# A two-block model on one core: norm gains by a product, early vectors, a split gate block, and ordered modulation additions

## The chip, the cores and the metric

The kernel runs on one core of a Trainium2 chip. The core has a matrix engine (TensorE, PE in the rows; its weight loads are PEld), VectorE (DVE), ScalarE (ACT), GpSimd (POOL) and SyncE (SP), which here issues almost all DMAs, in order. The metric is the device time of one execution in microseconds. The kernel before took 2379.94 us (median of three runs, 2379.12 to 2382.21). Where a clock is given, it is the share of TensorE's full speed that was granted in a stretch: 1.00 is 2.4 GHz, 0.50 is 1.2 GHz, and a value between them is a mixture of the two.

## What is computed

A first block with two layers (an even and an odd one) over 256 latent and 256 context tokens of width 1024 is followed by a second block. The change lies in the even layer and in helpers that all layers use. The even layer modulates a normed input, multiplies it with one wide matrix, and runs window attention and a gated linear recurrence (HGRN) on the parts:

```python
def even_mixer(h_ctx, h_lat, w_in, w_out, qk_g, sink, out_g, lb, cos, sin, need_ctx):
    p = split_parts(h_lat @ w_in, EVEN_PARTS)     # a_q a_k a_v b_q b_ff b_fb b_i b_g
    pc = project_parts(h_ctx, w_in, EVEN_PARTS, names)
...
    k_ctx = kv_heads(pc['a_k'], qk_g[1])          # rms_norm of each 64-wide head, times qk_g
    q_lat = apply_rope(attn_q_heads(p['a_q'], qk_g[0]), cos, sin)
    k_lat = apply_rope(kv_heads(p['a_k'], qk_g[1]), cos, sin)
    a_lat = window_attention(q_lat, k_lat, kv_heads(p['a_v']), k_ctx, v_ctx, sink)
...
    o_fw, _ = gla_chunked(q_l, k_fw, i_l, lf_fw, s_fw)          # 4 heads of 128
    o_bw, _ = gla_chunked(flip(q_l), flip(k_bw), flip(i_l), flip(lf_bw), s_bw)
    b_lat = gated_head_norm(o_fw + flip(o_bw), p['b_g'], out_g)  # rms_norm * out_g * silu(b_g)
    y_lat = jnp.concatenate([a_lat.astype(dt), b_lat.astype(dt)], axis=-1) @ w_out

def modulate(h, shift, scale):                    # shift, scale: chunks of silu(c) @ mod_w + mod_b
    return h * (1.0 + scale) + shift
```

Each layer ends with a gated FFN (`swiglu`) behind a second modulated norm. The modulation vectors are the products of two condition vectors with a 1024x6144 matrix for each layer (`mod_w`, and `w_ada` in the second block).

## The kernel before, in words

All products run as three matmuls of high and low parts (`mm3`, L188 to L190). A weight tile comes by `wload` (L176 ff.): SP loads `raw`, ScalarE casts it to `whi`, VectorE or (every fourth) GpSimd subtracts to `wlo`; four buffers of each. A tile scheduler orders each engine's instructions by priority, and the five engines meet by semaphores.

The even layer begins in `layer_even` (L1066). Rows of x and ctx are loaded, normed and transposed to `xT`. `modulate_first` (L1086) goes over the model width in four parts q, here called pairs, since each covers two chunks of 128: eight loads of mod_w (`mbig`, L1107, a buffer pool that holds two pairs), PE products of them with the conditions (L1112), the bias added on VectorE (`mrow`, L1118), a transposition (L1120), the modulation coefficients `firsta` and `firstb`, and the modulated operand chunks hi and lo. After each pair `first_products` (L1136) multiplies the two chunks with their rows of the weights. At q equal to 2 two DMAs spread the head-norm gains over all partitions (`qkg`, L1116). Ahead of pair 0 stand the loads of the norm vectors (L318) and of the modulation bias (`mbias`, L1097).

`even` (L706) then prepares q and k (`even_prep`, L945), makes gates for head pair 0 (`gates_in`), the values (`proj_narrow` with BI), and interleaves the four HGRN heads (`hgrn_head`, L823) with attention (`even_attention`, L989) by a string of steps; at the step g it makes the gates of pair 1. At the end the gates b_g are made (`ev_g`), multiplied with the gain `ogain` on GpSimd (L792), and with the heads' outputs on VectorE and GpSimd (L800), and PE transposes the products (L801). Then come the residual rows' transpositions (L1062) and the out projection.

The modulation vectors of later norms are summed in small pieces between other work: `mod_sums` (L364) loads a piece of 128x512 (`mraw`, four buffers), and VectorE adds it, scaled by a condition, to `macc` (L382). `fill` (L394), called by every `mm3`, advances it at a set rate. At a norm, `norm_sums` and `norm_spread` (L548 ff.) make the row norms and spread them over `nrs`; the first weight blocks of the FFN or of the next layer run on unnormed operands, and VectorE applies nrs to their results (`scaled`, L600, tile `nu`), while `normed` (L608) makes the normed operands: `nt` (L618), its high part on ScalarE, its low part `hTl` (L620).

Of the kernel before, what the change touches and what calls it, by code (L numbers as in the profile page):

```python
# [11 lines left out]
F32 = mybir.dt.float32  # L12
# [3 lines left out]
ALU = mybir.AluOpType  # L16
# [3 lines left out]
P = 128  # L20
D = 1024
# [74 lines left out]
class Net:  # L96
    def __init__(self, ctx, tc, I, out):
        self.ctx, self.tc, self.nc, self.I, self.out = ctx, tc, tc.nc, I, out
        self.n = 0
        e = ctx.enter_context  # L100
        self.cp = e(tc.tile_pool(name="cp", bufs=1, reuse_waits="tile"))
        self.wp = e(tc.tile_pool(name="wp", bufs=2))
        self.st = e(tc.tile_pool(name="st", bufs=4))
        self.mpool = e(tc.tile_pool(name="mp", bufs=1, reuse_waits="tile"))
        self.gran, self.pool_every = 0, 4
        self.credit, self.rate, self.todo = 0, 0, iter(())

# [173 lines left out]
    def setup(self):  # L281
        nc, I = self.nc, self.I
        self.vidx, self.vc = {}, self.t(self.cp, [P, 96], tag="vcols")
        flat = lambda a: a.rearrange("l (k p) -> (l k) p", p=P)
        self.vectors({"c": flat(I["c"]), "cc": I["c_ctx"].rearrange("(k p) -> k p", p=P), "c2": flat(I["c_2"])}, first=True)
        self.neghalf = self.t(self.cp, [P, 40], tag="neghalf")
        nc.gpsimd.memset(self.neghalf, -0.5)
        self.half = self.t(self.cp, [P, 4], tag="half")
        nc.gpsimd.memset(self.half, 0.5)
        self.ones2 = self.t(self.cp, [P, 2], tag="ones2")  # L290
        nc.gpsimd.memset(self.ones2, 1.0)
        self.onesq = self.t(self.cp, [P, P], tag="onesq")
        nc.gpsimd.memset(self.onesq, 1.0)

        sil = self.t(self.cp, [P, 24], tag="sil")
        nc.scalar.activation(sil, self.vc[:, 0:24], AF.Silu)
        self.cond = self.t(self.cp, [P, 8, 32], tag="cond")
        nc.gpsimd.memset(self.cond, 0.0)
        for m in range(2):
            nc.vector.tensor_copy(self.cond[:, :, m], sil[:, m * 8:m * 8 + 8])  # L300
        self.vs = [sil[:, o:o + 8] for o in (0, 8, 16)]
# [62 lines left out]
    def mod_sums(self, M, r):  # L364
# [6 lines left out]
        for g0 in range(0, 4, step):  # L371
            gs, accs = range(g0, g0 + step), {}
            for g in gs:
                for m in range(len(vs)):
                    accs[g, m] = self.t(self.mod_pool, [P, 512], tag="macc", bufs=4)
                for k in range(8):
# [3 lines left out]
                    for m, v in enumerate(vs):  # L380
                        if k:
                            nc.vector.scalar_tensor_tensor(accs[g, m], raw, v[:, k:k + 1], accs[g, m], ALU.mult, ALU.add)  # L382
                        else:
                            nc.scalar.activation(accs[g, m], raw, AF.Copy, scale=v[:, 0:1])
# [223 lines left out]
    def normed(self):  # L608
# [3 lines left out]
        with self.urgent():  # L612
            for k in range(8):
                for m, x in enumerate(self.nx):
# [4 lines left out]
                    nc.scalar.activation(hi[:, k, c], t, AF.Identity, bias=b)  # L619
                    nc.vector.scalar_tensor_tensor(lo[:, k, c], t, b, hi[:, k, c].bitcast(F32), ALU.add, ALU.subtract)  # L620
        self.ns.close()
# [84 lines left out]
    def even(self, products, ps, M, load, follow):  # L706
# [6 lines left out]
        with pool("ev") as op, ExitStack() as es:  # L713
# [7 lines left out]
            def gates_in(pair):  # L721
# [4 lines left out]
                for i, c0 in enumerate((BFF, BFB, BQ)):  # L726
                    wt = self.wfm(w, c0 + pair * 256)
                    for fb in range(2):
                        pa = self.acc()
                        self.fm_block(h, 0, 512, wt, fb, pa)  # L730
                        nc.scalar.activation(sg[fb][:, i] if i < 2 else q[fb], pa, AF.Copy, scale=1.0 if i < 2 else 0.5)
            hs = ExitStack()
            with pool("at") as ap:
                kT = self.t(ap, [P, 2, 2, 512], F32R, tag="kT")
                av = self.t(ap, [P, 4, P], tag="av")
                with pool("pp2") as pp, ps:
                    raw = products.send(av)
                    ke = self.const(op, "even")
                    imask = self.const(op, "imask")
                    self.setup_rest()  # L740
                    self.even_prep(pp, ke, raw, qT, kT)
# [12 lines left out]
                nc.vector.tensor_scalar(hi2, lb, 0.5, 0.5, ALU.mult, ALU.add)  # L754
                gates_in(0)
                with tc.high_priority(-1200):
                    for r in (1, 2):
                        self.mod_round(M, r, op)
                self.proj_narrow(h, TBS, w, BI, 512, lambda tb, c, pa: nc.scalar.copy(v[:, tb, c], pa))
                hp = hs.enter_context(pool("hg", side="right"))  # L760

                for nm, n in (("St", 896), ("A1", 1024), ("Bp1", 1024)):
                    self.t(hp, [P, n], tag=nm)
                with pool("sa") as sp:
                    head = lambda hd: self.hgrn_head(hp, ke, imask, hd, *src[hd], lo2, hi2, v)
                    heads = {0: head(0), 1: head(1)}
                    at = self.even_attention(sp, qT, kT, av, [2, 3, 0, 1])
                    for st in "000aa0aaag01111aa022aa12aaaa1aa33aa2aaaa2aa233a33":
                        if st == "a":
                            next(at, None)  # L770
                        elif st == "g":
                            with tc.high_priority(-800):
                                gates_in(1)
                            heads.update({2: head(2), 3: head(3)})
# [7 lines left out]
            with hs:  # L782
                gain = self.bcast_rows(yp, I["hgrn_out_norm_g"][0], P, "ogain")
                nc.vector.tensor_scalar(gain, gain, 0.5, None, ALU.mult)
# [203 lines left out]

    def even_attention(self, ap, qT, kT, av, tbs):  # L989

        nc, tc, I = self.nc, self.tc, self.I
        sink = self.bcast_rows(ap, I["attn_sink"][0], 8, "sink")
        nsink = self.t(ap, [P, 8], tag="nsink")
# [72 lines left out]
    def layer_even(self, M, load):  # L1066
# [7 lines left out]
        self.scratch([], None)  # L1074
        self.qkg = self.t(pp, [P, 10, 64], tag="qkg")
        xT = self.t(self.npool, [P, 8, 512], tag="xT")
        for tb in TBS:
            for i, pt in enumerate(self.norm_rows(src[tb], self.npool)):
                (self.nc.vector.tensor_copy if i else self.nc.scalar.copy)(xT[:, i * 4:i * 4 + 4, tb * P:tb * P + P], pt.rearrange("p (k t) -> p k t", t=P))
        first = self.modulate_first(M, xT)  # L1080
        products = self.first_products(first, I["even_w_in"][0], pp)
# [4 lines left out]
    def modulate_first(self, M, xT):  # L1086

        nc, I, cond = self.nc, self.I, self.cond
        flat = lambda a: a.rearrange("l (k p) -> (l k) p", p=P)
        self.vectors({"ng": I["norm_g"].rearrange("l s (k p) -> (l s k) p", p=P), "nm": flat(I["norm_mix_2"]),  # L1090
                      "nf": flat(I["norm_ffn_2"]), "lb": flat(I["hgrn_lb"])})
        gain = self.vcol("ng", 0)
        bias = self.t(self.npool, [P, 4, P], tag="mbias")
        nc.gpsimd.memset(bias, 0.0)
        for s in range(2):
            for m in range(2):
                nc.sync.dma_start(bias[s * 64:s * 64 + 64].rearrange("(j c) q n -> j c q n", c=32)[:, m],  # L1097
                                  M["bias"][s * D:s * D + D].rearrange("(q j n) -> j q n", j=2, n=P))
        A, B = (self.t(self.npool, [P, 8, 2], tag=nm) for nm in ("firsta", "firstb"))
        (hi, lo), h = self.fm_tiles()  # L1100
        for q in range(4):
            pa = self.bank("mod")
            for k0 in range(0, 8, 2):
# [4 lines left out]
                for i in range(2):  # L1108
                    for s in range(2):
                        for j in range(2):  # L1110
                            g = 64 * s + 32 * j
                            nc.tensor.matmul(pa[g:g + 32, :P], lhsT=cond[:, k0 + i], rhs=raw[:, i, s, j * P:j * P + P],  # L1112
                                             start=k0 + i == 0, stop=k0 + i == 7)
            if q == 2:
                for i, n0, n1 in ((0, 0, 8), (1, 8, 10)):
                    nc.sync.dma_start(self.qkg[:, n0:n1], I["attn_qk_norm_g"][0, i].unsqueeze(0).unsqueeze(0).to_broadcast([P, n1 - n0, 64]))  # L1116
            row = self.t(self.npool, [P, P], tag="mrow", bufs=2)
# [875 lines left out]
```

## Time and profile before

| | |
|---|---|
| median of three runs | 2379.94 us (2379.12 to 2382.21) |
| the profiled execution | 2377.75 us, its span 2375.9 us |
| busy: PE, DVE, ACT, POOL | 2258.2 (95%), 1612.3 (68%), 1064.4 (45%), 761.3 us (32%) |
| bytes moved | 396.70 MB, mean 167 GB/s |
| granted clock over the span | 0.978 |

The profile is of one execution. The first 400 of the 2376 us hold the first block's even layer up to its FFN. A busy share is an average over stretches with different limits, so the table of stretches below is the place to begin: a stretch in which PE is busy throughout has PE as its limit, one with holes has the work that the holes wait for. In a row of waits or of the timeline, the part in square brackets is the time for which the engine stood idle before that instruction, and what ended it.

### The profile page before, as it was taken

To read this page: it belongs to the slowest core of one execution; us is meant where nothing else is said; L and a number is where in the kernel's file an instruction comes from. 1 tells how busy PE (TensorE), PEld (TensorE's weight loads), DVE (VectorE), ACT (ScalarE), POOL (GpSimd) and SP (SyncE) were. 2 spreads that over 40 slices of the span, in tenths; PEclk is the share of its full clock that TensorE was granted. 3 is DMA by queue.
4 is the path that set the end of the run, shared out by engine and by line. 5 is a ranking of instruction groups with operands and counts; after the bars stand their busy time and mean duration, and the time that the engine had idled before them with its cause. 6 is when DMAs were issued, how large, how long until landed. Compare 5 with 4: busy or idle time off the path is not lost. (4 is left out here: it accounts for less than half of the span.)

```text
span 2375.9 us, 41450 instructions
## 1 busy us (share of the span) xinstructions
PE 2258.2 (95%) x16308; PEld 2018.6 (85%) x16308; DVE 1612.3 (68%) x2583; ACT 1064.4 (45%) x1754; POOL 761.3 (32%) x565
## 2 busy tenths in 40 slices
PE   6989989999999899988999899999999889999999
PEld 5767668777778788878999788999999788999999
DVE  2677858775557856568845978548765887548773
ACT  3555524332224433335445654445444655445443
POOL 1454432111012122213444663223223555224221
PEclk9989999999999999999999989999999999999999
DMA  7433335576666557575855634345666544355554
GB/s 247 147 102 113 125 114 161 157 225 209 192 196 210 182 175 238 153 232 171 281 184 167 177 89 121 115 151 162 187 182 185 160 130 114 107 148 172 178 182 138
DMA packets 352423, 396.70 MB, mean 167 GB/s; under 512 B 33916, under 2 KB 297004, under 8 KB 350180
## 3 DMA queue, kind: packets, MB, share of 16 engines
q1 hardware_dynamic: 350052, 393.92, 53.7%
q8 instruction: 128, 2.10, 0.4%
q14 instruction: 67, 0.55, 0.1%
q10 hardware_dynamic: 2176, 0.13, 0.1%
HBM read 390.28 MB, written 3.70 MB: 166 GB/s over the span
## 5 line engine op out<-in xcount | busy, mean ns | idle before, releaser
L180 ACT CAST whi<-raw 128x1024 fp32r<-128x1024 f32 (+2 forms) x536 | 551.5, 1034 | 598.3 <-PE acc L189 387.0
L182 POOL TENSOR_TENSOR wlo<-raw,whi 128x1024 fp32r<-128x1024 f32 (+1 forms) x168 | 411.0, 2446 | 1082.3 <-ACT whi L180 991.7
L188 PE MATMUL acc<-hTh,whi 128*128 128x256 f32 (+2 forms) x2256 | 693.0, 309 | 13.4 <-DVE nu L600 8.0
L182 DVE TENSOR_TENSOR wlo<-raw,whi 128x1024 fp32r<-128x1024 f32 (+1 forms) x368 | 482.0, 1310 | 329.1 <-ACT whi L180 328.1
L189 PE MATMUL acc<-hTl,whi 128*128 128x256 f32 (+2 forms) x2256 | 695.1, 309 | 7.7 <-DVE hTl L620 7.7
L190 PE MATMUL acc<-hTh,wlo 128*128 128x256 f32 (+2 forms) x2256 | 695.1, 309 | 4.3 <-DVE wlo L182 4.3
L188 PEld LDWEIGHTS acc<-hTh,whi 128*128 128x128 f32 x2256 | 430.5, 191 | 43.0 <-issue 9.8
L189 PEld LDWEIGHTS acc<-hTl,whi 128*128 128x128 f32 x2256 | 430.8, 191 | 31.0 <-DVE hTl L620 10.0
L190 PEld LDWEIGHTS acc<-hTh,wlo 128*128 128x128 f32 x2256 | 431.7, 191 | 28.7 <-DVE wlo L182 5.1
L382 DVE SCALAR_TENSOR_TENSOR macc<-mraw,sil,macc 128x512 f32<-128x512 f32 x280 | 249.2, 899 | 72.4 <-DMA mraw<-in_w_ada_dram 35.4
L189 PE MATMUL acc<-hidl,whi 128*128 128x256 f32 (+1 forms) x704 | 218.1, 310 | 0.0
L190 PE MATMUL acc<-hidh,wlo 128*128 128x256 f32 (+1 forms) x704 | 217.7, 310 | 0.0
L188 PE MATMUL acc<-hidh,whi 128*128 128x256 f32 (+1 forms) x704 | 217.6, 310 | 0.0
L188 PE MATMUL acc<-whi,hTh 128*128 128x512 f32 (+2 forms) x560 | 193.6, 347 | 6.8 <-DVE nu L600 2.2
L189 PE MATMUL acc<-wlo,hTh 128*128 128x512 f32 (+2 forms) x560 | 190.3, 341 | 2.7 <-POOL wlo L182 2.6
L190 PE MATMUL acc<-whi,hTl 128*128 128x512 f32 (+2 forms) x560 | 186.8, 343 | 2.8 <-DVE hTl L620 2.2
L188 PEld LDWEIGHTS acc<-hidh,whi 128*128 128x128 f32 x704 | 132.2, 188 | 9.7 <-issue 1.7
L190 PEld LDWEIGHTS acc<-hidh,wlo 128*128 128x128 f32 x704 | 132.6, 188 | 7.9
L189 PEld LDWEIGHTS acc<-hidl,whi 128*128 128x128 f32 x704 | 132.6, 188 | 7.9
L188 PEld LDWEIGHTS acc<-whi,hTh 128*128 128x128 f32 x560 | 107.2, 192 | 28.2 <-issue 8.1
L190 PEld LDWEIGHTS acc<-whi,hTl 128*128 128x128 f32 x560 | 105.8, 191 | 18.7 <-DVE hTl L620 4.4
L189 PEld LDWEIGHTS acc<-wlo,hTh 128*128 128x128 f32 x560 | 107.0, 191 | 15.6 <-POOL wlo L182 3.1
(559 smaller groups left out, 3787.0 us busy)
## 6 DMA issues: line engine op xcount, KB each, us to landing
raw<-in_w_in_dram SPq DMA_DIRECT2D x112, 512.0 KB
mraw<-in_w_ada_dram SPq DMA_DIRECT2D x192, 256.0 KB
raw<-in_ffn_w_in_dram SPq DMA_DIRECT2D x88, 512.0 KB
raw<-in_w_up_dram SPq DMA_DIRECT2D x88, 512.0 KB
mraw<-in_mod_w_dram SPq DMA_DIRECT2D x96, 256.0 KB
raw<-in_odd_w_in_dram SPq DMA_DIRECT2D x48, 512.0 KB
raw<-in_ffn_w_out_dram SPq DMA_DIRECT2D x40, 512.0 KB
raw<-in_w_down_dram SPq DMA_DIRECT2D x40, 512.0 KB
```

Source lines behind the costliest of these rows:

```text
L180: nc.scalar.copy(hi, raw)
L182: eng.tensor_tensor(lo, raw, hi.bitcast(F32), ALU.subtract)
L188: mm(out, lhsT=ah, rhs=bh, start=start, stop=False)
L189: mm(out, lhsT=ah, rhs=bl, start=False, stop=False)
L190: last = mm(out, lhsT=al, rhs=bh, start=False, stop=stop)
L382: nc.vector.scalar_tensor_tensor(accs[g, m], raw, v[:, k:k + 1], accs[g, m], ALU.mult, ALU.add)
```

## The change

The head-norm gains come as one row of 128 numbers into a zeroed 128x128 tile (`qkrow`); a product with a matrix of ones spreads it over the partitions, and two copies on ScalarE write `qkg`. The norm vectors and the modulation bias are issued behind the eight `mbig` loads of pair 0 instead of ahead of them. The broadcasts of `ogain` and `sink` move from where they are used to the constants ahead of `even_prep`. `gates_in` becomes a generator; its first third for pair 1 (BFF, two weight tiles, 48 products) is made right behind the values, the rest at the step g as before. `normed` records its last low-part instruction as `fence`, and each VectorE addition of `mod_sums` that is issued later is ordered behind it. A column tile (`neghalf`) shrinks from 40 to 16 columns.

```diff
@@ mod_sums
                         if k:
-                            nc.vector.scalar_tensor_tensor(accs[g, m], raw, v[:, k:k + 1], accs[g, m], ALU.mult, ALU.add)
+                            add = nc.vector.scalar_tensor_tensor(accs[g, m], raw, v[:, k:k + 1], accs[g, m], ALU.mult, ALU.add)
+                            if self.fence is not None:
+                                self.after(add, self.fence)
@@ normed
-                    nc.vector.scalar_tensor_tensor(lo[:, k, c], t, b, hi[:, k, c].bitcast(F32), ALU.add, ALU.subtract)
+                    self.fence = nc.vector.scalar_tensor_tensor(lo[:, k, c], t, b, hi[:, k, c].bitcast(F32), ALU.add, ALU.subtract)
@@ even: gates_in, constants, values, heads
+                    yield
...
                     imask = self.const(op, "imask")
+                    gain = self.bcast_rows(op, I["hgrn_out_norm_g"][0], P, "ogain")
+                    sink = self.bcast_rows(op, I["attn_sink"][0], 8, "sink")
...
-                gates_in(0)
+                for _ in gates_in(0):
+                    pass
...
                 self.proj_narrow(h, TBS, w, BI, 512, lambda tb, c, pa: nc.scalar.copy(v[:, tb, c], pa))
+                gates = gates_in(1)
+                next(gates)
...
                             with tc.high_priority(-800):
-                                gates_in(1)
+                                for _ in gates:
+                                    pass
...
             with hs:
-                gain = self.bcast_rows(yp, I["hgrn_out_norm_g"][0], P, "ogain")
@@ even_attention
-        sink = self.bcast_rows(ap, I["attn_sink"][0], 8, "sink")
@@ layer_even
+        qk = self.t(pp, [P, 2, 64], tag="qkrow")
+        self.nc.gpsimd.memset(qk, 0.0)
+        self.nc.sync.dma_start(qk[0:1], I["attn_qk_norm_g"])
...
+        pq = self.sm()[:, :P]
+        self.nc.tensor.matmul(pq, lhsT=self.onesq, rhs=qk.rearrange("p a d -> p (a d)"), start=True, stop=True)
+        for i, n0, n1 in ((0, 0, 8), (1, 8, 10)):
+            self.nc.scalar.copy(self.qkg[:, n0:n1], pq[:, i * 64:i * 64 + 64].unsqueeze(1).to_broadcast([P, n1 - n0, 64]))
@@ modulate_first
-            if q == 2:
-                for i, n0, n1 in ((0, 0, 8), (1, 8, 10)):
-                    nc.sync.dma_start(self.qkg[:, n0:n1], I["attn_qk_norm_g"][0, i].unsqueeze(0).unsqueeze(0).to_broadcast([P, n1 - n0, 64]))
+            if q == 0:
+                self.vectors({"ng": I["norm_g"].rearrange("l s (k p) -> (l s k) p", p=P), "nm": flat(I["norm_mix_2"]),
+                              "nf": flat(I["norm_ffn_2"]), "lb": flat(I["hgrn_lb"])})
+                gain = self.vcol("ng", 0)
...
```

How this moves instructions is seen at three places. On SP, in the even layer's prologue; mbig is mod_w, raw from L176 a weight tile. Before:

```order
L1107 DMA mbig_498<-in_mod_w_dram 128x2x256 x2
L1107 DMA mbig_509<-in_mod_w_dram 128x2x256 x2
L1116 DMA qkg_113<-in_attn_qk_norm_g_dram 128x8x64
L1116 DMA qkg_113<-in_attn_qk_norm_g_dram 128x2x64
L176 DMA raw_540<-in_even_w_in_dram 128x2x512
L1107 DMA mbig_571<-in_mod_w_dram 128x2x256 x2
```

And now, where the same two mbig loads are followed by the weight tile at once:

```order
L1114 DMA mbig_505<-in_mod_w_dram 128x2x256 x2
L1114 DMA mbig_516<-in_mod_w_dram 128x2x256 x2
L176 DMA raw_545<-in_even_w_in_dram 128x2x512
L1114 DMA mbig_576<-in_mod_w_dram 128x2x256 x2
L1114 DMA mbig_587<-in_mod_w_dram 128x2x256 x2
```

The two qkg loads are gone from between them. On VectorE at the even FFN's norm (macc is a modulation addition, nt a normed operand, nu the first results scaled). Before:

```order
L563 TENSOR_SCALAR nsum_3746<-k_ident_79,rr_628_3743 128x128 x4
L382 SCALAR_TENSOR_TENSOR macc_4087<-mraw_4182,sil_92,macc_4087 128x512
L382 SCALAR_TENSOR_TENSOR macc_4086<-mraw_4199,sil_92,macc_4086 128x512
L182 TENSOR_TENSOR wlo_4063<-raw_4060,whi_4062 128x1024
L382 SCALAR_TENSOR_TENSOR macc_4212<-mraw_4227,sil_92,macc_4212 128x512
L382 SCALAR_TENSOR_TENSOR macc_4087<-mraw_4199,sil_92,macc_4087 128x512
L382 SCALAR_TENSOR_TENSOR macc_4213<-mraw_4227,sil_92,macc_4213 128x512
L618 SCALAR_TENSOR_TENSOR nt_3992<-x_3228,moda_3438,nrs_3780 128x256
```

And now:

```order
L565 TENSOR_SCALAR nsum_3751<-k_ident_79,rr_630_3748 128x128 x4
L620 SCALAR_TENSOR_TENSOR nt_3997<-x_3233,moda_3443,nrs_3785 128x256
L620 SCALAR_TENSOR_TENSOR nt_4001<-c_3261,moda_3445,nrs_3785 128x256
L620 SCALAR_TENSOR_TENSOR nt_4005<-x_3233,moda_3443,nrs_3785 128x256
L620 SCALAR_TENSOR_TENSOR nt_4009<-c_3261,moda_3445,nrs_3785 128x256
L602 TENSOR_TENSOR nu_3787<-acc_3712,nrs_3785 128x256
```

No addition stands between nsum and nt any more; the same additions follow behind the norm's operands, in runs of 9 to 12 with single weight tiles between them. On GpSimd at the end of the even stage (sg is a gate block, sq a head's output, rv and rr the last head's row norms). Before, all multiplications with ogain stand together, ahead of the first gated output and of the last head's norm:

```order
L792 TENSOR_TENSOR sg_519_2924<-sg_519_2924,ogain_2921 128x256 x2
L792 TENSOR_TENSOR sg_520_2925<-sg_520_2925,ogain_2921 128x256 x2
L792 TENSOR_TENSOR sg_519_2924<-sg_519_2924,ogain_2921 128x256 x2
L792 TENSOR_TENSOR sg_520_2925<-sg_520_2925,ogain_2921 128x256 x2
L800 TENSOR_TENSOR sq_177_921<-sq_177_921,sg_519_2924 128x128
L800 TENSOR_TENSOR sq_178_922<-sq_178_922,sg_519_2924 128x128
L159 TENSOR_SCALAR rv_514_2907<-ss_513_2905 128x4
```

And now only the last head's norm and its gated outputs are left there, behind the last of the attention's softmax rows (P):

```order
L800 TENSOR_TENSOR sg_522_2930<-sg_522_2930,ogain_756 128x256
L1023 TENSOR_SCALAR P_2606<-P_2606,es_478_2609 128x512
L407 MEMSET mraw_1236 128x512
L159 TENSOR_SCALAR rv_517_2914<-ss_516_2912 128x4
L533 MEMSET bz_585_3447 128x16
L533 MEMSET bz_586_3452 128x16
L161 TENSOR_TENSOR rr_518_2916<-rv_517_2914,neghalf_84 128x4
L808 TENSOR_TENSOR sq_252_1481<-sq_252_1481,sg_521_2929 128x128
L808 TENSOR_TENSOR sq_252_1481<-sq_252_1481,sg_522_2930 128x128
```

On PE the transpositions of the first two heads' gated outputs accordingly stand ahead of the last head's products, and the early third of pair 1's gates stands right behind the values, but behind the product that waits for `A` (L882 before, L890 now), which has kept its place.

## Rows read from the trace of the kernel before

**Rows 1.** The page: the span of the profiled execution.
```profile
span 2375.9 us, 41450 instructions
```
**Rows 2.** Stretches: length, busy PE PEld DVE ACT POOL, granted clock, DMA share, GB/s.
```profile
59.40:137.50 78.10, 66.44 (x411) 53.51 (x412) 57.44 (x80) 43.70 (x73) 42.70 (x25) 0.92 0.41 133
137.50:310.60 173.10, 172.04 (x1360) 127.93 (x1358) 126.72 (x305) 83.10 (x184) 77.53 (x62) 0.99 0.37 119
310.60:334.70 24.10, 14.63 (x97) 10.68 (x97) 14.71 (x33) 5.08 (x11) 11.02 (x21) 0.79 0.28 95
...
399.35:440.00 40.65, 39.81 (x207) 33.21 (x208) 40.50 (x75) 21.27 (x41) 3.23 (x3) 0.95 0.50 154
440.00:800.00 360.00, 356.98 (x1639) 287.79 (x1637) 233.79 (x318) 116.42 (x176) 54.96 (x34) 1.00 0.63 198
```
**Rows 3.** Timeline of SP's queue, 31 to 45 us: start, duration of the issue, what.
```profile
31.30 2.11 SPq L1116 DMA_DIRECT2D qkg<-in_attn_qk_norm_g_dram  x2
33.45 1.14 SPq L176 DMA_DIRECT2D raw<-in_even_w_in_dram  x1
34.69 9.77 SPq L1107 DMA_DIRECT2D mbig<-in_mod_w_dram  x1
```
**Rows 4.** Busy time by stretch, prologue, columns as in the second group.
```profile
30.00:36.00 6.00, 6.00 (x43) 4.52 (x43) 2.74 (x3) 1.14 (x2) 0.00 (x0) 1.00 0.98 305
36.00:46.00 10.00, 9.63 (x96) 7.85 (x95) 2.90 (x8) 2.08 (x4) 0.00 (x0) 1.00 0.14 34
...
52.40:59.40 7.00, 3.15 (x13) 2.79 (x14) 1.42 (x4) 2.03 (x5) 2.17 (x1) 0.74 1.06 360
```
**Rows 5.** Timeline of VectorE, 44 to 64 us.
```profile
48.12 0.29 DVE L1118 TENSOR_TENSOR mrow<-mod,mbias 128x128 f32<-128x128 f32 x1 [7.81 <-PE mod L1112]
```
**Rows 6.** Timeline of PE, 30 to 64 us.
```profile
36.94 0.27 PE L1120 MATMUL mod<-k_ident,mrow 128*128 128x128 f32 x1
...
39.02 0.50 PE L188 MATMUL acc<-whi,hTh 128*128 128x512 f32 x1
...
62.13 0.61 PE L188 MATMUL acc<-whi,hTh 128*128 128x512 f32 x1
62.58 0.39 PE L189 MATMUL acc<-wlo,hTh 128*128 128x512 f32 x1
62.80 0.40 PE L188 MATMUL acc<-whi,hTh 128*128 128x512 f32 x1
```
**Rows 7.** Waits of PE, 100 to 140 us: total, times, longest (us).
```profile
PE rc L882 <- DVE A L864: 8.5, 1, 8.5
```
**Rows 8.** Timeline of POOL, 316 to 328 us.
```profile
317.33 5.70 POOL L792 TENSOR_TENSOR sg<-sg,ogain 128x256 f32<-128x256 f32 x8 [3.66 <-DVE ogain L784]
```
**Rows 9.** Waits of PE, 310 to 336 us.
```profile
PE sm L801 <- POOL sq L800: 6.9, 3, 4.9
```
**Rows 10.** Timeline of PE, 328 to 335 us.
```profile
328.74 0.47 PE L801 MATMUL sm<-k_ident,sq 128*128 128x128 f32 x1 [1.85 <-POOL sq L800]
...
334.71 0.48 PE L188 MATMUL acc<-qT,whi 128*128 128x512 f32 x1
```
**Rows 11.** Timeline of ACT, 393 to 395 us.
```profile
394.04 0.59 ACT L575 COPY nrs<-sm 128x512 f32<-128x512 f32 x1
```
**Rows 12.** Groups of VectorE's instructions, 378 to 412 us: count, busy us, mean ns.
```profile
L382 DVE SCALAR_TENSOR_TENSOR macc<-mraw,sil,macc 128x512 f32<-128x512 f32 x28 | 21.5, 815 | 0.4 <-DMA mraw<-in_mod_w_dram 0.3
```
**Rows 13.** Timeline of VectorE, 392 to 400 us.
```profile
393.13 4.16 DVE L382 SCALAR_TENSOR_TENSOR macc<-mraw,sil,macc 128x512 f32<-128x512 f32 x3 [0.27 <-DMA mraw<-in_mod_w_dram]
397.21 0.47 DVE L618 SCALAR_TENSOR_TENSOR nt<-x,moda,nrs 128x256 f32<-128x256 f32 x1
...
398.79 1.07 DVE L600 TENSOR_TENSOR nu<-acc,nrs 128x256 f32<-128x256 f32 x3
```
**Rows 14.** Timeline of PE, 392 to 402 us.
```profile
399.35 0.55 PE L188 MATMUL acc<-hTh,whi 128*128 128x258 f32 x1 [5.35 <-DVE nu L600]
```
**Rows 15.** Waits of PE, 440 to 830 us.
```profile
PE acc L188 <- DVE nu L600: 3.2, 3, 1.3
```

More of the change, by code (lines that the diff above doesn't have):

```diff
@@ L105, in __init__ @@
         self.gran, self.pool_every = 0, 4
-        self.credit, self.rate, self.todo = 0, 0, iter(())
+        self.credit, self.rate, self.todo, self.fence = 0, 0, iter(()), None
     def t(self, pool, shape, dtype=F32, tag=None, bufs=None):
@@ L285, in setup @@
         self.vectors({"c": flat(I["c"]), "cc": I["c_ctx"].rearrange("(k p) -> k p", p=P), "c2": flat(I["c_2"])}, first=True)
-        self.neghalf = self.t(self.cp, [P, 40], tag="neghalf")
+        self.neghalf = self.t(self.cp, [P, 16], tag="neghalf")
         nc.gpsimd.memset(self.neghalf, -0.5)
@@ L766, in even @@
                     heads = {0: head(0), 1: head(1)}
-                    at = self.even_attention(sp, qT, kT, av, [2, 3, 0, 1])
+                    at = self.even_attention(sp, sink, qT, kT, av, [2, 3, 0, 1])
                     for st in "000aa0aaag01111aa022aa12aaaa1aa33aa2aaaa2aa233a33":
@@ L987, in even_prep, with even_attention @@
                 nc.vector.tensor_copy(qT[:, half * 4:half * 4 + 4, tb * P:tb * P + P], pq.rearrange("p (h t) -> p h t", t=P))
-    def even_attention(self, ap, qT, kT, av, tbs):
+    def even_attention(self, ap, sink, qT, kT, av, tbs):
         nc, tc, I = self.nc, self.tc, self.I
-        sink = self.bcast_rows(ap, I["attn_sink"][0], 8, "sink")
         nsink = self.t(ap, [P, 8], tag="nsink")
@@ L1089, in modulate_first @@
         flat = lambda a: a.rearrange("l (k p) -> (l k) p", p=P)
-        self.vectors({"ng": I["norm_g"].rearrange("l s (k p) -> (l s k) p", p=P), "nm": flat(I["norm_mix_2"]),
-                      "nf": flat(I["norm_ffn_2"]), "lb": flat(I["hgrn_lb"])})
-        gain = self.vcol("ng", 0)
         bias = self.t(self.npool, [P, 4, P], tag="mbias")
         nc.gpsimd.memset(bias, 0.0)
[L1095 to L1098, printed above, removed]
         A, B = (self.t(self.npool, [P, 8, 2], tag=nm) for nm in ("firsta", "firstb"))
@@ L1113, in modulate_first @@
                                              start=k0 + i == 0, stop=k0 + i == 7)
-            if q == 2:
-                for i, n0, n1 in ((0, 0, 8), (1, 8, 10)):
-                    nc.sync.dma_start(self.qkg[:, n0:n1], I["attn_qk_norm_g"][0, i].unsqueeze(0).unsqueeze(0).to_broadcast([P, n1 - n0, 64]))
+            if q == 0:
+                self.vectors({"ng": I["norm_g"].rearrange("l s (k p) -> (l s k) p", p=P), "nm": flat(I["norm_mix_2"]),
+                              "nf": flat(I["norm_ffn_2"]), "lb": flat(I["hgrn_lb"])})
+                gain = self.vcol("ng", 0)
+                for s in range(2):
+                    for m in range(2):
+                        nc.sync.dma_start(bias[s * 64:s * 64 + 64].rearrange("(j c) q n -> j c q n", c=32)[:, m],
+                                          M["bias"][s * D:s * D + D].rearrange("(q j n) -> j q n", j=2, n=P))
             row = self.t(self.npool, [P, P], tag="mrow", bufs=2)
```

## The prediction

> **What bounds the kernel now.** I read the span first [rows 1], then a table of busy time by stretch, then the waits of each stretch in which TensorE (PE) has a hole, and last what the queues do in it. The table [rows 2] shows where the even layer's holes are: between 59.4 and 137.5 us PE is busy 66.44 of 78.1 us, between 310.6 and 334.7 only 14.63 of 24.1 us at a granted clock of 0.79, while 137.5 to 310.6 (172.04 of 173.1) and 440 to 800 (356.98 of 360) are full. A step that ends earlier in a full stretch carries its gain to the end, and an instruction that a full stretch gets in addition costs its duration.
>
> The prologue before 59.4 has a hole of its own. SP issues the two qkg loads at 31.30 and then needs 9.77 us for the issue of one mbig load [rows 3]. What the core moves falls from 305 GB/s (30 to 36) to 34 GB/s (36 to 46), while PE still lives on what landed before (9.63 of 10 us busy); later, from 52.4 to 59.4, PE is busy 3.15 of 7 us, at a clock of 0.74 [rows 4]. The weights that lie behind the two loads on SP, the casts that wait for them on ACT, and PE behind these, are all late by the length of the drought.
>
> **The change part by part.** Durations are of one execution of 2377.75 us, 1.85 us more than its span [rows 1]; the median of the runs shown is 2379.94, 2.19 us more, which I add at the end.
>
> *Prologue.* The two qkg loads (128x10 copies of one 256-byte row, 1280 pieces) go; a load of one row comes instead, with one 128-column product and two ACT copies. The drought goes with them, if they made it. PE then starts the third pair of input chunks when the products of the second pair are through. VectorE adds the bias to the third pair's mod columns at 48.12 in 0.29 us, after a wait for PE alone [rows 5], so the columns are there on time already. Some copies on ACT and a product behind them stand ahead of the transposition on PE: 1 us, a guess from the 0.59 us of one ACT copy of 128x512 [rows 11]. For the second pair the transposition stood at 36.94 and the first product of the pair came at 39.02 [rows 6], 2.1 us later. So the third pair may start at 48.4 + 1 + 2.1 = 51.5, where it now starts at 62.13 [rows 6]: 10.6 us, and up to 0.5 more for the stretch in which the clock stood low. I take 11. Weights are no new limit: 36 to 46 moves 0.34 MB, at 305 GB/s it would be 3 MB, so the loads come as much earlier as PE does. Ends: 8 (a wait for weights of some 3 us stays) and 14 (62.13 - 48.4, the transposition and operands hidden too).
>
> Vectors and mbias behind the first eight mbig loads: the same copies go through the same queue, only later, and the first bias addition then waits for them instead of for mod_w. I take 0, from -2 to +3.
>
> The wait of 8.5 us for A from VectorE L864 [rows 7], the largest in the stretch 59.4 to 137.5, stays: VectorE's order ahead of that instruction is unchanged and its chain starts from the same products, so it moves with them. The added product and copies stand where PE and ACT wait for loads anyhow: 0, at most 1.1 us (0.27 as the transposition [rows 6], and ACT's 0.59 and a quarter of it for the smaller copy).
>
> *ogain and sink early.* At the end of the even stage the gain's row lands late: POOL starts its eight multiplications at 317.33, after 3.66 us of waiting for ogain, needs 5.70 us, and only then the outputs' gates (L800) [rows 8]; PE waits 6.9 us for them in three pieces, the longest 4.9 [rows 9]. Now the multiplications stand earlier on POOL, before the last head's end, as the order rows show. What is late next is head 3's own chain (its norm rv, rr, then its gates), which already ends the last wait of 1.85 us at 328.74 [rows 10]. Without the 3.66 us of waiting and 5.70 of multiplying POOL would be ready 9.4 us sooner; the last head's chain permits no such gain, since its transpositions need rr after its last product. PE's transpositions of heads 0 and 1 (8 x 0.27, 2 us) move ahead of the last head's products, and the waits of 6.9 go but for about 1: 6 us. Ends: 2 (only the wait for ogain less what head 3's norm needs) and 9 (POOL's whole 9.4).
>
> *The fence.* At the even FFN's norm VectorE does 28 modulation additions (21.5 us) between 378 and 412 [rows 12]. Three of them, 393.13 to 397.2, lie between PE's sums and the operand nt; nrs, which nt also needs, is written by ACT at 394.04 to 394.63 [rows 11]. nt takes four steps of 0.40, nu starts at 398.79 [rows 13] and PE, idle for 5.35 us, at 399.35 [rows 14]. With the additions behind the operands VectorE can start nt at 394.65, so nu at 396.25 and PE at 396.8: 2.55 us. A part of what the low clock costs there may go too (0.95 over 40.65 us [rows 2], at most 2 us): I take 3, from 0 to 4.6. At the three later norms the same waits are smaller: in the stretch from 440 to 830 nu costs PE 3.2 us in three pieces [rows 15]. I take 2 for all later norms, from -2 to 5.
>
> *A part of the gates sooner.* The same weights and 48 products, one every 0.22 to 0.23 us [rows 6] (11 us), are done right behind BI instead of among the heads. The order rows show that they don't stand ahead of the products that wait for A, so they fill no hole: both places lie in the stretch that is 172.04 of 173.1 busy. The first head's scores come 11 us later on PE, and 173 us of full PE stand behind them. 0, from -8 (the last head ends later and its chain is bare) to +3.
>
> Sum: 11 + 0 + 6 + 3 + 2 + 0 = 22 us. 2377.75 - 22 = 2355.75, and with 2.19 **2358 us**. Its own range is 2350 to 2366.
>
> The Trainium skill has a rule that speaks against the first term: its page "DMA: Bandwidth & Descriptors", section "Why small descriptors are slow (HBM only)", counts a fixed handful of cycles for each packet, so that 256-byte pieces cost only some 27% over large ones. By that 320 KB would be an estimated 1.2 us of the queue, and the drought would have another cause. The rows do not agree: at 34 GB/s for ten microseconds, directly behind the two issues, the queue passes far less than 256-byte pieces would by that rule.
>
> **The rivals.**
>
> *The drought isn't the broadcast's.* If the 9.77 us have another cause (mbig's buffers, or a completion that SP waits for), they stay. For it: SP's long issue is of an mbig load, not of qkg. Against it: the low rate begins when the loads ahead of qkg are through, and the load that is issued so long is one of the fourth pair, which takes the buffers of the second; that pair's products begin at 39.02 [rows 6], so PE had read these buffers by then, and the issue ends at 44.46. Then 10.5 of the 22 us go: about 2368.
>
> *Won ahead, given back at the wait for A.* VectorE is busy 57.44 and POOL 42.70 of 78.1 us there [rows 2]; if their chain to L864 is bound by work that doesn't start from the products (constants, mod rounds), PE waits the longer: 8.5 + 11. Against it: POOL and VectorE wait for PE's results at its start. About 2369.
>
> *Slower: the additions come back as lumps.* From 399.35 to 440 VectorE is busy 40.50 of 40.65 us [rows 2]. The additions held back don't vanish: they stand in lumps of 9 to 12, at 21.5 / 28 = 0.77 us [rows 12] 7 to 9 us each, ahead of low parts of weights (wlo) that PE needs. Their four buffers stay full meanwhile, and SP, which issues in order, holds weight loads behind the next modulation load. PE lives on four weight tiles, about two blocks of 11 us. If a lump at each of the four norms outlasts that by its 7 us, 28 us are lost and the fence's 5 not won: 2358 + 33 = 2391. It is slower than before from a loss of 17 / 4, about 4.3 us, at each norm. Against it: VectorE is busy 233.79 of 360 us in the stretch behind [rows 2], so a lump has room soon.
>
> *The gates help.* If an earlier second pair lets heads 2 and 3 start before PE runs dry at 310, the tail shrinks by the whole 24.1 - 14.63 = 9.5 us instead of 6, and the clock there rises from 0.79: 5 to 8 us more, about 2351.
>
> **How the numbers follow.** Forecast 0.62; the drought stays 0.06; given back at the wait for A 0.10; gates help 0.12; lumps 0.06; a milder loss that leaves the time where it was 0.04. From 2343 (gates help, and the prologue at its upper end) to 2372 (both middle rivals, with 3 us for what they leave over) about 0.82 is held. A change under 0.2%, 4.8 us, cannot be told from none here. The first four cases are faster but for their tails (0.03, to the same and the slower side): 0.87; same, the milder loss with two of the tail: 0.06; slower, the lumps and the rest: 0.07.
>
> **What would show it.** In the changed profile: no long issue of an mbig load on SP and no stretch at 34 GB/s; the third pair's first product near 51; the wait for A of L872 still 8 to 9 us, near 122; PE's out projection about 17 us earlier than 334.71 [rows 10]; PE's wait for nu at the FFN's norm 2 to 3 us; no wait for wlo of several us in the 40 us behind each norm. The forecast is wrong if the low stretch stays, if the wait for A grows by the gain, or if PE waits for wlo or whi behind the norms.

## The result and the profile after

The changed kernel took 2347.81 us (median of four runs, 2343.62 to 2351.05) beside 2381.07 us for the kernel before in the same comparison (2379.12 to 2385.20): a ratio of 0.9856, 95% interval 0.9838 to 0.9874, faster by 33 us. The forecast was 2358, with a range of 2343 to 2372. The direction and the range held; the sum of 22 us was a third too small, and its terms were less right than the sum: the prologue's is near, the two that were put at nothing hold, the 6 us for ogain are nothing, and the 5 us for the fence are 18 to 20. That the range held is in part luck: the 6 us too many made up for some of the 13 to 15 too few.

Where the time came from is read best as a lead. Each product of PE in one trace is matched with the same product in the other (by its operands' names, and its count among those of that name), and the median of the differences is taken over a stretch (where the kernel before is at 900 us, for example, the changed kernel does the same product 18.9 us sooner):

| at (us, kernel before) | lead of the changed kernel (us) | what lies ahead of it |
|---|---|---|
| 130 | 7.1 | prologue |
| 340 | 6.9 | even stage with its end |
| 450, then 650 | 17.5, then 14.7 | even FFN's norm |
| 900 | 18.9 | odd layer's norm |
| 1090 | 26.7 | end of the odd layer's mixer |
| 1125, then 1250 | 30.9, then 24.0 | odd FFN's norm |
| 1600 | 31.9 | second block's first layer |
| 2340 | 34.0 | the rest |

The changed kernel's profile is of its fastest execution (2343.62 us), so the last 34 us are one more than the medians differ by.

The prologue, first SP's queue in the changed kernel (start, duration of the issues, how many) and then the same stretches as in [rows 4] and the first three of [rows 2] by the lead (length; busy PE, PEld, DVE, ACT, POOL; clock, DMA share, GB/s):

```profile
32.66 0.37 SPq L176 DMA_DIRECT2D raw<-in_even_w_in_dram  x1
33.50 2.58 SPq L1114 DMA_DIRECT2D mbig<-in_mod_w_dram  x4
```

```profile
36.00:46.00 10.00, 10.00 (x79) 8.27 (x78) 2.91 (x8) 3.02 (x5) 2.38 (x1) 1.00 1.08 370
...
52.40:59.40 7.00, 6.56 (x83) 4.76 (x84) 5.34 (x12) 3.50 (x6) 0.00 (x0) 1.00 0.49 152
...
130.45:303.70 173.25, 168.68 (x1320) 125.66 (x1322) 127.61 (x303) 81.90 (x182) 86.46 (x76) 0.97 0.35 116
303.70:327.85 24.15, 20.62 (x140) 13.39 (x133) 12.66 (x34) 5.92 (x13) 4.31 (x8) 0.84 0.32 110
```

No issue is long any more, and the stretch that moved 34 GB/s moves 370. The last row is the end of the even stage: 24.15 us as before, though PE is busy 20.62 instead of 14.63 us of it.

Waits of PE from 0 to 150 us, from 150 to 400, from 760 to 830 and from 1060 to 1210 (total, times, longest):

```profile
PE rc L890 <- DVE A L872: 8.5, 1, 8.5
...
PE sm L809 <- POOL sq L808: 3.2, 1, 3.2
...
PE acc L188 <- DVE nu L602: 2.3, 1, 2.3
...
PE acc L190 <- DVE wlo L182: 4.3, 3, 2.8
...
PE acc L189 <- DVE hTl L622: 1.3, 1, 1.3
...
PE acc L188 <- ACT hTh L621: 0.5, 1, 0.5
```

The wait for A is the 8.5 us of [rows 7]; the wait for the gated outputs is less than half of [rows 9]; between 150 and 400 us there is no wait for nu at all, where the even FFN's norm had cost 5.35 us [rows 14]; and the wait for wlo behind the odd FFN's norm is the one that a rival had named.

### The profile page after: what moved, and what is told of

The parts are those of the page before. It is cut to its first block, busy times and chain, and to the rows that moved or that the text cites. A ratio compares the mean times of both kernels' runs of the same rounds, so it can differ in the third digit from the quotient of the medians.

```text
span 2341.8 us, 41459 instructions
## 1 busy us (share of the span) xinstructions
PE 2250.1 (96%) x16310; PEld 2010.8 (86%) x16310; DVE 1617.4 (69%) x2583; ACT 1060.5 (45%) x1754; POOL 764.1 (33%) x566
## 5 line engine op out<-in xcount | busy, mean ns | idle before, releaser
L182 POOL TENSOR_TENSOR wlo<-raw,whi 128x1024 fp32r<-128x1024 f32 (+1 forms) x168 | 416.8, 2481 | 1034.4 <-ACT whi L180 964.5
```

What stands on the lines that cost most here:

```text
L182: eng.tensor_tensor(lo, raw, hi.bitcast(F32), ALU.subtract)
```

## The experiments

Each kernel was timed beside runs of the kernel before on the same chip; for each its median is given, and its ratio to before with the 95% interval. Executions of one kernel lie up to 10 us apart, so two kernels within some 4 us are not told apart.

**The gains broadcast again** (undone alone).

```diff
...
-        self.nc.sync.dma_start(qk[0:1], I["attn_qk_norm_g"])
...
+            if q == 2:
+                for i, n0, n1 in ((0, 0, 8), (1, 8, 10)):
+                    nc.sync.dma_start(self.qkg[:, n0:n1], I["attn_qk_norm_g"][0, i]...to_broadcast([P, n1 - n0, 64]))
```

> The changed kernel with the two broadcast loads of the head-norm gains back where they were (behind the third pair's mod_w loads), instead of the row, its product and the two copies. Theory: the broadcast alone makes the drought. In the changed kernel the third pair's first product came at 54.61 us; here a stretch of some 10 us under 50 GB/s returns, the third pair starts near 64, and the whole is 9 to 11 us slower than the changed kernel (about 2357). Rival: the long issue of the mod_w load has another cause that the earlier vectors removed; then no drought, and within 3 us of the changed kernel.

Measured 2358.76 us, ratio 0.9902 (0.9884 to 0.9921): 11 us slower than the changed kernel. SP's queue and the stretches, in this kernel:

```profile
32.42 2.17 SPq L1124 DMA_DIRECT2D qkg<-in_attn_qk_norm_g_dram  x2
34.68 1.07 SPq L176 DMA_DIRECT2D raw<-in_even_w_in_dram  x1
35.85 12.27 SPq L1107 DMA_DIRECT2D mbig<-in_mod_w_dram  x3
```

```profile
36.00:46.00 10.00, 9.63 (x110) 7.72 (x109) 3.20 (x9) 2.08 (x4) 0.00 (x0) 1.00 0.10 30
```

The drought is back with the two loads, and the third pair starts at 65.16 us instead of 54.61. The first rival of the prediction (another cause) is out. What in these loads is slow is not shown: no run tells the number of their pieces, 1280, from the fact that all of them are read from two short rows.

**Vectors and bias ahead again** (undone alone).

```diff
-            if q == 0:
-                self.vectors({"ng": ...
...
+        self.vectors({"ng": ...
...
```

> The changed kernel with the loads of the norm vectors and of the modulation bias ahead of the first pair's mod_w loads again. Theory: the late vectors cost the changed kernel time at the start (the first transposition of modulation columns came at 25.81 us, before the change at 23.99): here it comes near 24.0, the gain is 2 to 3 us at the wait for A, and the whole is 2 to 3 us faster than the changed kernel (about 2345). Rival: the short loads take their 2 us of the queue in either place and only the place of the hole differs: no difference beyond 1 us.

Measured 2348.56 us, ratio 0.9865 (0.9845 to 0.9885): no difference. Its profile does lead that of the changed kernel by 2.5 us at 140 us; but the next two kernels, whose prologue is the changed kernel's, lead it there by 4.1 and 2.0 us. The start of an execution scatters, and I had read a cause into it.

**ogain and sink late again** (undone alone).

```diff
-                    gain = self.bcast_rows(op, I["hgrn_out_norm_g"][0], P, "ogain")
...
+                gain = self.bcast_rows(yp, I["hgrn_out_norm_g"][0], P, "ogain")
```

> The changed kernel with ogain and sink loaded late again. Theory (the prediction's): the early gain saves the wait at the end of the even stage; with it late, POOL's eight multiplications stand in one block there and PE waits 6 to 7 us for the gated outputs: 4 to 6 us slower than the changed kernel. Rival: the end of the even stage is set by the last heads, which came 9 us later in the changed kernel because of the moved gates or of the multiplications now among the heads; if it is the multiplications, this kernel is no slower than the changed one.

Measured 2352.48 us (2348.81 to 2356.25), ratio 0.9879 (0.9858 to 0.9900). The median fits the theory, but its place does not: against the changed kernel this one's lead is 4.1 us at 140 us, 4.2 us at 340 and 4.1 us at 1300 us. The even stage loses nothing by the late gain; what it loses comes in the second block, which the edit doesn't touch, where the kernels with the gains, the vectors or the gates undone lose 4 to 6 us against the same profile too. Its slower executions have no profile; that the late gain costs nothing is borne out by the kernel with two edits alone, below, which has it late and takes 2349.05 us.

**The gates in one piece again** (undone alone).

```diff
-                gates = gates_in(1)
-                next(gates)
...
-                                for _ in gates:
+                                for _ in gates_in(1):
```

> The changed kernel with all of the second pair's gates at the step g again. In the changed kernel PE's lead over before was 6.9 us at 140 us and 6.9 us at 340 us, so the end of the even stage gained nothing though the wait for the gated outputs fell from 6.9 to 3.2 us. Theory: the moved third of the gates puts the heads back by what the early gain wins; here the out projection starts 4 to 7 us earlier than the 327.87 us of the changed kernel and the whole is 4 to 7 us faster (about 2342). Rival: the gates' place is worth nothing (the prediction's value) and the out projection starts within 1.5 us of 327.9.

Measured 2348.49 us, ratio 0.9863 (0.9842 to 0.9884): no difference; the lead against the changed kernel is 2.0 us at 140 and 2.3 us at 340 us. My theory was wrong: the gates' place is worth nothing to the whole.

**No fence** (undone alone).

```diff
-                            if self.fence is not None:
-                                self.after(add, self.fence)
```

> The changed kernel without the order between the modulation additions and the norm's last low part. Theory: of the 34 us between the two profiles 6.9 come from the prologue and nearly all the rest from this order (lead 6.9 us at 340 us, 24 us at 1300, 34 at the end): without it the lead stays near 7 us and the whole is 17 to 27 us slower than the changed kernel (2365 to 2375), with waits for nu of some 5 us at the even FFN's norm. Rival (the prediction's size): the order is worth 5 us, and the rest is the scheduler's other orders, which the layout and the earlier prologue changed: 3 to 8 us slower (about 2354).

Measured 2367.73 us, ratio 0.9952 (0.9940 to 0.9963): 20 us slower than the changed kernel. The waits of PE from 375 to 440 us in this kernel:

```profile
PE acc L188 <- DVE nu L600: 3.0, 1, 3.0
PE acc L189 <- DVE hTl L620: 2.8, 1, 2.8
```

Both are gone with the fence. Against the changed kernel's profile it is 2.9 us behind at 340 us; this grows by 7.5 us at the even FFN's norm, by 2.5 at the odd layer's, by 7 from the end of the odd mixer to behind the odd FFN's norm, and by 9 in the second block, where the three kernels above, which keep the fence, also fell 4 to 9 us behind that profile: of these 9 a part, perhaps all, is scatter. The profiled execution, 2372.53 us, is the slowest of five, so the 29 us at its end are more than the 20 between the medians.

**The fence alone**, on the kernel before (the three edits of the diff in `mod_sums` and `normed`).

> The kernel before with this order alone. Theory: it brings 17 to 27 us by itself (2355 to 2364), beginning at the even FFN's norm (8 us). Rival: 3 to 8 us (2374 to 2378).

Measured 2362.66 us, ratio 0.9924 (0.9911 to 0.9937): 18 us faster than before. Its lead is below zero at 340 us (it began 1.8 us late), 6.0 us at 600, 10.3 at 900, 17.6 at 1090, 21.6 at 1125 and 13.4 at 1250 us. Two experiments from either side agree: the fence is worth 18 to 20 us, not the 5 of the prediction.

**The fence behind the fourth chunk, or the first.**

```diff
-                    self.fence = nc.vector.scalar_tensor_tensor(lo[:, k, c], ...
+                    low = nc.vector.scalar_tensor_tensor(lo[:, k, c], ...
+                    if k < 4:
+                        self.fence = low
```

> The changed kernel with the additions ordered behind the fourth of the eight chunks of a norm's operands instead of behind the last. In the changed kernel each norm gives back a part of its gain to lumps of additions behind it (2.8 us at the even FFN, 7 us at the odd FFN between 1140 and 1220 us). Theory: the additions then lie among the later chunks, which PE needs later, the lumps get smaller, and the whole is 3 to 10 us faster than the changed kernel (2338 to 2345). Rival: VectorE is full through the operands, the additions delay the later chunks and PE waits for hTl: 0 to 8 us slower.

> The changed kernel with the additions ordered behind the first chunk's operands only. Theory: what the order brings is that nt and nu, which stand between the norm's sums and PE, are not held up; then most of the gain stays (within 6 us of the changed kernel). Rival: the later chunks' operands need the cover as well; 8 us or more slower, with PE waiting for hTl.

Measured 2355.41 us, ratio 0.9896 (0.9883 to 0.9909), and 2361.14 us, ratio 0.9917 (0.9904 to 0.9931) with `k < 1`: 8 and 13 us slower than the changed kernel. The rivals hold; with the first chunk PE waits 3.4 us for hTl at the even FFN and 3.7 at the odd one. The waits of PE from 1060 to 1210 us with the fourth chunk:

```profile
PE acc L190 <- DVE wlo L182: 6.5, 4, 2.5
PE acc L189 <- DVE hTl L622: 2.6, 1, 2.6
PE acc L188 <- ACT hTh L621: 1.8, 1, 1.8
```

Against the rows of the changed kernel above hTl and hTh cost more, and wlo does not cost less: earlier additions delay the later operands and relieve nothing behind them.

**Two edits alone**: the kernel before with the gains by a product and the fence.

> The kernel before with two of the changed kernel's edits: the head-norm gains by a row and a product, and the modulation additions behind the norm's operands. Vectors, ogain, sink and gates stay as before. Theory: these two are the whole change: undone alone they cost 11 and 20 us, undone alone the other three cost between 1 and 5 us, within what the runs scatter; here 11 + 18 = 29 us faster than before, 2350 to 2353, within 5 us of the changed kernel. Rival: the other three edits bring together what none shows alone (late vectors and an early gain, or gates and gain): 2356 or more.

Measured 2349.05 us (2347.33 to 2349.88), ratio 0.9874 (0.9857 to 0.9890): 30 us faster than before, 1.2 us from the changed kernel by the medians and some 4 by the ratios. Within what the runs tell apart, these two are the whole change. Its end of the even stage, waits of PE from 290 to 336 us:

```profile
PE sm L803 <- POOL sq L802: 6.9, 3, 4.8
```

It waits as long as [rows 9], and still its lead at 340 us is 7.2 us where the changed kernel's is 6.9.

**Short additions.**

```diff
-  ...scalar_tensor_tensor(accs[g, m], raw, v[:, k:k + 1], accs[g, m], ...)
+  ...scalar_tensor_tensor(accs[g, m][:, 0:32], raw[:, 0:32], v[:, k:k + 1], accs[g, m][:, 0:32], ...)
```

> The changed kernel with each modulation addition done on 32 of its 512 columns (the other columns keep the first piece alone, so later modulation vectors are not those of the reference): the same instructions and the same loads, but each addition takes some 0.1 instead of 0.7 us of VectorE. Theory: what each norm gives back behind it is VectorE's time in additions ahead of wlo; the waits for wlo of 4.3 us between 1140 and 1200 us go, and the whole is 8 to 14 us faster than the changed kernel (2334 to 2340). Rival: it is the loads of the pieces, which now come while the FFN's weights are loaded (286 to 303 GB/s there): within 4 us of the changed kernel, with the same waits behind the odd FFN's norm.

Measured 2350.30 us (2344.65 to 2353.12), ratio 0.9879 (0.9864 to 0.9893): no faster. An addition takes 0.25 us here instead of 0.75, a third and not the 0.1 us that I had expected. Behind the odd FFN's norm the theory holds; waits of PE from 1060 to 1210 us:

```profile
PE acc L190 <- DVE wlo L182: 1.4, 1, 1.4
```

2.9 us of the 4.3 are gone, and the kernel gains 6 us on the changed one between 1130 and 1190 us. But it loses 3.7 us around 425 us, 3 around 935 us and 7 between 1300 and 1450 us. At the first two PE waits 1.9 us for act on ScalarE and 2.1 us for rt on VectorE; the changed kernel doesn't wait there. So what is given back at the odd FFN is VectorE's time; the losses elsewhere have other causes. The scheduled order of this kernel differs too, and which of order and loads makes them stays open.

## Why the prediction came out as it did

**Prologue, 11 us: near.** The step is right: the broadcast makes the drought, and undoing it alone costs 11 us. In the profile the lead was 7.1 us; the seven profiles with the same prologue lead by 6.3 to 11 us at 140 us, 8.3 in the mean. So the size was some 3 us high in the mean, no more than the start scatters. The third pair started at 54.61 instead of 51.5:

```profile
37.67 0.27 PE L1132 MATMUL mod<-k_ident,mrow 128*128 128x128 f32 x1
...
52.47 0.33 PE L1132 MATMUL mod<-k_ident,mrow 128*128 128x128 f32 x1 [0.39 <-DVE mrow L1130]
...
54.61 0.50 PE L188 MATMUL acc<-whi,hTh 128*128 128x512 f32 x1
```

The second pair's transposition stood at 36.94 before [rows 6]; the changed profile was late already there. PE had products of the second pair to do until 51.5 and the third pair's modulation products behind them, so the third pair's transposition came at 52.47; from there to the first product it is the 2.1 us of the forecast.

The rule weighed against this term, of the Trainium skill's page "DMA: Bandwidth & Descriptors", section "Why small descriptors are slow (HBM only)", counts 3 of the 11 cycles of a 256-byte piece as overhead, 27%. The run with the broadcast back moved 30 GB/s in these ten microseconds, a tenth of the 310 GB/s of the six ahead of them, so here the measurement decides against it.

**Vectors 0, gates 0, the wait for A unchanged: right**, each by a run or a row. The early third of the gates filled no hole, as the order had said.

**ogain early, 6 us: wrong, it is 0.** The failed step is "the last head's chain ... already ends the last wait": I shortened the tail behind the last head and left the last head where it was. The wait for the gated outputs fell from 6.9 to 3.2 us (forecast: to about 1), but the last head came later, and the out projection starts 6.8 us earlier than before instead of the 17 that were named as a sign. Its last product and what follows, in the kernel before (first two lines: timeline of PE, the last product and the longest of the waits for the gated outputs) and in the changed one:

```profile
316.69 0.38 PE L936 MATMUL rc<-St,sq 128*64 128x128 f32 x2
323.55 1.15 PE L801 MATMUL sm<-k_ident,sq 128*128 128x128 f32 x4 [4.85 <-POOL sq L800]
```

```profile
318.55 0.38 PE L944 MATMUL rc<-St,sq 128*64 128x128 f32 x2
...
323.19 0.44 PE L809 MATMUL sm<-k_ident,sq 128*128 128x128 f32 x2 [3.23 <-POOL sq L808]
...
327.87 0.48 PE L188 MATMUL acc<-qT,whi 128*128 128x512 f32 x1
```

With the lead of 6.9 us the last product should have come near 309.8; it came at 318.55, 8.7 us late, and the tail behind it is 9.3 instead of 18.0 us. What makes the last head late is seen in the stretches from the wait for A to its last product, before and in the changed kernel (columns as in [rows 2]):

```profile
137.50:317.20 179.70, 177.17 (x1404) 130.93 (x1402) 128.38 (x311) 83.19 (x185) 78.06 (x63) 0.99 0.38 125
```

```profile
130.45:319.10 188.65, 184.04 (x1414) 134.62 (x1413) 134.28 (x319) 83.97 (x187) 88.41 (x77) 0.95 0.36 121
```

Ten transpositions of gated outputs have come in from behind. PE is idle for 4.6 instead of 2.5 us. And the clock is 0.95 instead of 0.99, some 7 us: PE runs at half clock from about 301 to 311 us, among the last heads, where the kernel before had such a stretch from 322 to 332 us, behind them (0.50 from 304 to 308 here, from 324 to 328 there). Why the low clock comes sooner no run shows.

Which edit holds the heads up can be read from the other profiles. By each one's lead at 135 us its last head comes 8 to 10 us late in the seven with early gain and split gates, 5 us with early gain alone, 2.5 us with split gates alone, and 0.5 us with neither (the two kernels made from the one before). What each wins behind the last head it loses ahead: the four combinations take the time of the kernel before from 140 to 340 us, within 0.6 us. (Two of the seven, without the fence and with the fourth chunk, lose 2.4 and 2.0 us there, with a second stretch of low clock.)

**Fence at the even FFN, 3 us: too small, it is 8.** The mechanism is the one forecast. What I missed stands ahead of the place I looked at. The rows of the changed kernel at this norm (PE, ACT, DVE):

```profile
382.10 1.06 PE L573 MATMUL sm<-nsum,onesq 128*128 128x128 f32 x8
```

```profile
383.19 0.59 ACT L577 COPY nrs<-sm 128x512 f32<-128x512 f32 x1 [2.56 <-PE sm L573]
```

```profile
383.81 0.48 DVE L620 SCALAR_TENSOR_TENSOR nt<-x,moda,nrs 128x256 f32<-128x256 f32 x1 [3.58 <-ACT nrs L577]
...
385.40 0.75 DVE L602 TENSOR_TENSOR nu<-acc,nrs 128x256 f32<-128x256 f32 x2
```

By the lead of 6.9 us the spreading product, at 392.95 before, should have come at 386.1; it came at 382.1. The additions had also stood ahead of `nsum`, so this product had been put behind all weight products; now 4 us of weight products follow it (382.91 to 386.96), and they cover nrs and nu wholly. I had counted three additions between nrs and nu (2.55 us) out of the 28 of [rows 12], and taken PE's order as given. The same work of PE before and now, from 340 to 450 us before:

```profile
340.00:450.00 110.00, 103.81 (x542) 87.41 (x541) 93.87 (x155) 50.70 (x97) 21.82 (x17) 0.97 0.52 159
```

```profile
333.10:432.50 99.40, 99.40 (x533) 85.28 (x532) 71.01 (x123) 48.21 (x93) 20.53 (x17) 1.00 0.41 130
```

The 6.2 us in which PE was idle are gone, 5.35 of them the wait for nu, and so is the stretch of low clock behind that wait, some 2 us. The lead of 17.5 us at 450 us holds 2 us more that are not won: eight products that sum macc over the partitions (L388 before, L390 now) stood at 414.8 us and come at 443.3 us in the changed kernel, behind the additions. When they are done the lead is 15.1.

**Fence at the later norms, 2 us: too small, and the place is another one.** With the fence alone on the kernel before, the lead grows by 4 us at the odd layer's norm, by 7.5 at the end of the odd layer's mixer, where there is no norm, falls by 4 over the odd FFN's norm (4 up, 8 down), and grows by 2 behind it. Without the fence 18 are lost behind the even FFN, with the scatter of the second block in them. This term and the last are where the missing third of the sum lies. I had priced it by the waits for nu alone, 3.2 us [rows 15], which all belong to the odd layer's norm.

What I didn't see is at the end of the odd mixer, ahead of the FFN's norm: the stretch before, the additions in it, and the same stretch now.

```profile
1048.00:1072.00 24.00, 17.90 (x102) 15.89 (x101) 16.69 (x23) 8.54 (x15) 6.00 (x7) 0.79 0.84 279
```

```profile
L382 DVE SCALAR_TENSOR_TENSOR macc<-mraw,sil,macc 128x512 f32<-128x512 f32 x13 | 9.8, 756 | 5.3 <-DMA mraw<-in_w_ada_dram 5.0
```

```profile
1029.00:1045.50 16.50, 13.83 (x100) 12.52 (x100) 7.50 (x10) 7.81 (x14) 4.81 (x6) 1.00 0.46 150
```

Thirteen additions for the second block stood among the mixer's last operands, PE was idle for 6.1 us (4.9 of them for oy, the gated output, L1255) and the clock was 0.79. Now no addition stands there, PE is idle for 2.7 us, and the clock is 1.00. All ten kernels with the fence have no addition there and 2.3 to 3.2 us of idle PE; the two without it have thirteen, and 6.1 and 9.0 us.

**The rivals.** The lumps exist, but not at the even FFN: there PE waits for nothing behind the norm. At the odd FFN's norm they outweigh what the fence brings: the lead is 26.7 us ahead of it and 24.0 behind it, and it falls over this norm by 2.7 to 8.3 us in every kernel with the fence but the one with short additions, where it grows by 2.7; without the fence it falls by 1.1. Of the 7 us that are given back in the changed kernel some 3 are longer waits for wlo, some 2 the low clock behind them (0.96 from 1139 to 1184 us), and the rest are small products done later than before. The rival's sum of 28 us was wrong: of the three norms of the first block that the additions reach only this one loses. The gates do not help, and nothing was given back at the wait for A.

**The range.** Its lower end was named as the gates' help together with the prologue's upper end; by the prediction's own figures these give 2358 - 8 - 3 = 2347, not 2343.

## What to carry to other kernels

When large loads queue behind a row that many partitions need, try spreading it by a product with ones instead of a broadcast load: here the broadcast was 320 KB, cost ten microseconds of the queue, and showed as the long issue of a later load. Where an in-order engine serves a critical chain and filler work, look for the filler ahead of the whole chain, back to its first sum and into the stage ahead of it, and let the scheduler place the chain anew before pricing a wait. A wait taken out behind a full stretch is worth nothing if the stretch's last producer comes later by as much: price the end of the stage, not the wait. And before calling a falling lead a loss, look for work that has only moved.

## What was not expected of the hardware

Two broadcast loads of 1280 pieces of 256 bytes were issued in 2.1 us, and then the queue moved only 30 to 34 GB/s for 10 us, by an estimate from these numbers about 8 ns a piece. What showed it was the issue of a later mod_w load: 9.77 us in the kernel before, and 12.27 us for three such issues in the kernel with the broadcast back. The start of an execution scatters: kernels with the same instructions in the prologue differ by up to 4.7 us at 140 us, which is as much as most of the small edits could bring.
